# Seven block products for eight in twelve of the 22 up pairs of a feed-forward

## The chip, the cores and the metric

The kernel runs on one core of a Trainium2 chip. The metric is the device time of one execution in microseconds; the median of three runs is 1257.51 us (1257.15 to 1257.99).

## The reference, cut to what matters

A gated-linear-attention block with its own feed-forward and norm comes first; then two layers on 256 latent and 256 context tokens of width 1024, each an attention mixer and a gated feed-forward, both modulated by six vectors that are made from the conditioning. Weights and activations are fp32. The change lies in the feed-forward of the first of these two layers (layer 0), which runs over both token sets, and in the last modulation set of layer 1.

```python
FFN_HIDDEN = ((8 * D_MODEL + 2) // 3 + 255) // 256 * 256      # 2816

def swiglu_ffn(h, w_in, w_out):
    a, g = jnp.split(h @ w_in, 2, axis=-1)
    return (jax.nn.silu(a) * g) @ w_out

for i in range(DEPTH_2):
    mod_l = (silu_c @ ada_w[i] + ada_b[i])[:, None, :]
    mod_c = (silu_cc @ ada_w[i] + ada_b[i])[None, None, :]
    ...
    h = h + g1_l * y_l
    h = h + g2_l * swiglu_ffn(ada_norm(h, norm_ffn[i], sh2_l, sc2_l), ffn_w_in[i], ffn_w_out[i])
    if ctx_out:
        hc = hc + g1_c * y_c
        hc = hc + g2_c * swiglu_ffn(ada_norm(hc, norm_ffn[i], sh2_c, sc2_c), ffn_w_in[i], ffn_w_out[i])
return rms_norm_2(h, norm_final)
```

## The kernel before

**Weights.** All weights stream through one list of units of 128 x 1024 numbers (512 KB), in the order in which they are used (`UNITS`). `w_load` issues their DMAs on SP into five `raw` buffers, four units ahead; `w_split` turns each into a high part `wh` (a cast on ScalarE, line 178) and a low part `wl` (a subtraction on VectorE, line 179), both fp32r, in twelve `w` buffers; `wnext` hands the next unit to the matmuls and splits up to `cap[0]` units ahead. Each product of two fp32 blocks is three fp32r matmuls (`mm3`, lines 193 to 195): high by high, low by high, high by low.

**Layer 0's feed-forward.** The hidden width 2816 is 22 blocks of 128. For each block f a pair of "f" units holds the columns of the a half and of the g half. `ffn_up` multiplies each unit, as the stationary operand, with the transposed tokens `fT` (256 latent columns, then 256 context columns): 8 blocks of K, three matmuls each, 512 columns. `ffn_act` makes silu(a) times g (lines 1111, 1112) and splits it (1118, 1119). `ffn_up_first` does the first two pairs in two halves of 256 columns. The 22 blocks go in two parts of 11; after each part `ffn_down0` multiplies them with the "h" units of the down matrix (two blocks of 128 rows by 512 columns; the eleventh block is a half unit) into one PSUM bank per token tile, and `gated` adds the result, times the gate, to the residual (1080, 1081). In the first part all four token tiles go together; in the second the context tiles (2, 3) come first and then, with the units loaded again, the latent ones (0, 1).

**Modulation.** `ada_jobs` makes the modulation vectors beside all this: each step loads 512 KB of `ada_w` into one of two `ada` buffers (line 304, on SP) and multiplies and sums it on VectorE (line 324), once per conditioning vector. `ada_run(adaC, n)` issues n steps. Sets 2 and 5 are gates, which `ada_finish` transposes on TensorE (348), stores as a row in DRAM and `load_gates` broadcasts back.

**Layer 1's feed-forward** runs on the latent tokens alone: in each of its turns `ffn_up` makes one pair of 256 columns and `mm_r` and `mm_h` one down unit of 512.

**Order.** The program is written in source order; outside the sections marked `manual_schedule` a planner sets the order on each engine, by source order and by what it takes to be ready, and may move independent steps ahead. On the chip each engine then keeps its order. A tile pool (`t2`, 58 buffers of 2 KB) holds nearly all else; PSUM has eight banks.

## Time and profile before

| | |
|---|---|
| median of three runs | 1257.51 us |
| the profiled execution | 1256.72 us, its span 1254.9 us |
| TensorE busy | 1244.0 us, 99% of the span |
| VectorE, ScalarE busy | 919.9 us (73%), 688.2 us (55%) |
| DMA | 231.22 MB, mean 184 GB/s |

The span runs from the first to the last instruction. Layer 0's feed-forward takes from about 575 to 940 us of it: up to 703 the first part's up pairs, to 760 its down products, to some 873 the second part's up pairs, then its down products. Matmuls are pipelined, so the duration shown for one (0.28 or 0.40 us) is longer than the step from its start to the next one's.

### The profile page before, as it was taken

To read this page: it belongs to the slowest core of one execution; us is meant where nothing else is said; L and a number is where in the kernel's file an instruction comes from. 1 tells how busy PE (TensorE), PEld (TensorE's weight loads), DVE (VectorE), ACT (ScalarE), POOL (GpSimd) and SP (SyncE) were. 2 spreads that over 40 slices of the span, in tenths; PEclk is the share of its full clock that TensorE was granted. 3 is DMA by queue.
4 is the path that set the end of the run, shared out by engine and by line. 5 is a ranking of instruction groups with operands and counts; after the bars stand their busy time and mean duration, and the time that the engine had idled before them with its cause. 6 is when DMAs were issued, how large, how long until landed. Compare 5 with 4: busy or idle time off the path is not lost.

```text
span 1254.9 us, 18667 instructions
## 1 busy us (share of the span) xinstructions
PE 1244.0 (99%) x6872; PEld 1043.2 (83%) x6872; DVE 919.9 (73%) x1638; ACT 688.2 (55%) x1344; POOL 78.7 (6%) x137
## 2 busy tenths in 40 slices
...
GB/s 304 189 151 237 192 289 268 271 277 246 198 249 111 105 110 118 160 197 118 213 177 206 259 266 249 205 100 102 197 204 76 113 84 131 219 187 185 186 185 34
DMA packets 68507, 231.22 MB, mean 184 GB/s; under 512 B 8048, under 2 KB 8736, under 8 KB 68416
## 3 DMA queue, kind: packets, MB, share of 16 engines
...
## 4 chain that ended last, share of the span: by engine, by line
PE 95%; ACT 2%; DVE 1%; issue 1%; DMA 0%; POOL 0%; SPq 0%; POOLq 0%; ACTq 0%
PE b L193 28%; PE b L194 28%; PE b L195 28%; PE b L1000 2%; PE b L1469 1%; PE b L981 1%; PE b L232 1%; PE b L1455 1%; PE b L562 1%; PE b L962 1%; PE b L963 1%; PE b L951 1%; PE b L1436 1%; DVE wl L179 0%; DMA t<-in_xt_dram 0%
## 5 line engine op out<-in xcount | busy, mean ns | idle before, releaser
L178 ACT CAST wh<-raw 128x1024 fp32r<-128x1024 f32 (+1 forms) x308 | 320.7, 1045 | 392.8 <-PE b L194 292.4
L179 DVE TENSOR_TENSOR wl<-raw,wh 128x1024 fp32r<-128x1024 f32 (+1 forms) x308 | 372.5, 1216 | 154.9 <-ACT wh L178 151.9
L193 PE MATMUL b<-t,wh 128*128 128x256 f32 (+1 forms) x1120 | 365.7, 327 | 0.0
L194 PE MATMUL b<-t,wl 128*128 128x256 f32 (+1 forms) x1120 | 365.6, 327 | 0.0
L195 PE MATMUL b<-t,wh 128*128 128x256 f32 (+1 forms) x1120 | 365.3, 327 | 0.0
L193 PE MATMUL b<-wh,t 128*128 128x512 f32 (+1 forms) x748 | 299.2, 402 | 1.2 <-ACT t L250 0.6
L194 PE MATMUL b<-wh,t 128*128 128x512 f32 (+1 forms) x748 | 294.8, 394 | 0.0
L195 PE MATMUL b<-wl,t 128*128 128x512 f32 (+1 forms) x748 | 294.7, 394 | 0.0
L193 PEld LDWEIGHTS b<-t,wh 128*128 128x128 f32 x1120 | 210.7, 188 | 22.2
L194 PEld LDWEIGHTS b<-t,wl 128*128 128x128 f32 x1120 | 210.8, 188 | 21.9
L195 PEld LDWEIGHTS b<-t,wh 128*128 128x128 f32 x1120 | 210.5, 188 | 20.4 <-DVE t L251 0.2
L195 PEld LDWEIGHTS b<-wl,t 128*128 128x128 f32 x748 | 140.4, 188 | 34.2
L193 PEld LDWEIGHTS b<-wh,t 128*128 128x128 f32 x748 | 140.4, 188 | 32.2 <-ACT t L250 1.0
L194 PEld LDWEIGHTS b<-wh,t 128*128 128x128 f32 x748 | 140.8, 188 | 30.1 <-DVE t L251 0.5
L324 DVE CUSTOM_DVE_ANT_0 a<-a,crow 128x1024 f32<-128x1024 f32 x96 | 117.6, 1233 | 28.8 <-DMA a<-in_ada_dram 28.3
L324 DVE CUSTOM_DVE_ANT_0 t<-a,crow 128x1024 bf16<-128x1024 f32 x64 | 78.5, 1237 | 7.3 <-DMA a<-in_ada_dram 7.1
L1112 DVE TENSOR_TENSOR t<-b,t 128x512 f32<-128x512 f32 (+1 forms) x42 | 23.7, 564 | 59.4 <-PE b L195 52.2
L205 POOL TENSOR_TENSOR c<-c,mhalf 128x1 f32<-128x1 f32 x21 | 14.2, 676 | 539.0 <-DVE c L204 538.9
L339 POOL TENSOR_TENSOR mod<-mod,bcol 128x8 f32<-128x8 f32 x20 | 13.4, 671 | 475.1 <-DVE mod L324 472.7
L1118 ACT CAST t<-t 128x512 fp32r<-128x512 f32 (+1 forms) x42 | 21.7, 516 | 28.6 <-DVE t L1112 28.6
L212 ACT ACTIVATE t<-t 128x512 f32<-128x512 f32 x40 | 24.8, 624 | 10.8 <-DVE t L1081 6.4
L1445 ACT ACTIVATE t<-b,c,c 128x512 f32<-128x512 f32 x32 | 26.0, 812 | 3.5 <-POOL c L1443 3.5
...
## 6 DMA issues: line engine op xcount, KB each, us to landing
raw<-in_wst_dram SPq DMA_DIRECT2D x310, 512.0 KB, 4.4
a<-in_ada_dram SPq DMA_DIRECT2D x96, 512.0 KB, 4.4
...
crow<-in_cvec_dram SPq DMA_DIRECT2D x2, 512.0 KB
```

The lines of the kernel that those rows point to most:

```text
L178: A.copy(out=h[:, :n], in_=raw[:, :n])
L179: V.tensor_tensor(out=l[:, :n], in0=raw[:, :n], in1=h[:, :n], op=ALU.subtract)
L193: T.matmul(o, lhsT=lh, rhs=rh, start=first, stop=False)
L194: T.matmul(o, lhsT=ll, rhs=rh, start=False, stop=False)
L195: T.matmul(o, lhsT=lh, rhs=rl, start=False, stop=last)
L205: G.tensor_tensor(out=ms[:, 3:4], in0=ms[:, 2:3], in1=mhalf[:, 0:1], op=ALU.pow)
L212: A.activation(out=junk[hf], in_=halves[hf], func=AF.Square, scale=1.0 / 32.0, accum_out=ms[:, hf:hf + 1])
L324: V.tensor_tensor_reduce(out=raw if ci == n_c - 1 else t2([D], BF16), in0=raw, in1=crow[ci], scale=1.0, scalar=0.0, op0=ALU.mult, op1=ALU.add,
L1000: T.matmul(po[e * 64:(e + 1) * 64, cols_], lhsT=v, rhs=probs[(head, "l" if lat_q else "c")][:, c, :], start=(c == 0), stop=(c == n_c - 1))
L1112: V.tensor_tensor(out=a, in0=pg_[:, :n], in1=a, op=ALU.mult)
L1118: A.copy(out=h, in_=a)
L1445: A.activation(out=pl, in_=sl, func=AF.Exp, scale=r, bias=mx[:, 1:2], accum_out=mx[:, 2:3])
```

## The change

The up products of pairs 10 to 21 are computed by Winograd's form of Strassen's scheme on a 2 x 2 by 2 x 2 grid: the a and the g unit are the two rows, the two halves of K the inner index, latent and context tokens the two columns. Seven products of block sums take the place of eight products of blocks; a product is 4 blocks of K by three matmuls by 256 columns. `pair_sums` makes the sums of the weights one pair ahead and splits them; `token_sums` makes the sums of the tokens once, from the unsplit tokens that `to_T` now also keeps in `fX`; `ffn_up7` runs the seven products into three banks and combines them on ScalarE and VectorE. The tokens lie in two sets of tiles, `fL` and `fC`, so a plain pair becomes two runs of 256 columns. The 22 blocks go in three parts of 8, 8 and 6, without half units; two more rounds of gated sums follow from that, and 28 down units are loaded instead of 36. The steps of the sets in `adaC` are spread anew, and layer 1's set 5 (`adaD`) is made in the first turns of layer 1's down loop, with its gates loaded at f = 12. Not shown below: `mm3` gets a flag that lets a group of matmuls add onto an earlier one, and the width of a split is always 1024.

```diff
-HALF = NFT // 2
+PARTS = ((0, 8), (8, 16), (16, 22))
+F_SEVEN = 10
...
-    for part in range(2):
-        for f in range(part * HALF, (part + 1) * HALF):
+    for lo, hi in PARTS:
+        for f in range(lo, hi):
             u += [("f", "ffn_in0", P * f), ("f", "ffn_in0", FH + P * f)]
-        dn = [("h", "ffn_out0", part * HALF + f, 512 * h) for h in range(2) for f in range(0, HALF, 2)]
-        u += dn if part == 0 else dn + dn
+        dn = [("h", "ffn_out0", f, 512 * h) for h in range(2) for f in range(lo, hi, 2)]
+        u += dn if hi < NFT else dn + dn
...
+    def seven(u):
+        return u[1] == "ffn_in0" and u[2] % FH >= P * F_SEVEN
...
-        while wpos[1] < len(UNITS) and wpos[1] - wpos[2] + 1 < cap[0]:
+        while wpos[1] < len(UNITS) and wpos[1] - wpos[2] + 1 < cap[0] and not seven(UNITS[wpos[1]]):
...
-    adaC = ada_jobs([(0, 5, True), (1, 0, True), (1, 1, True)] + [(1, v, False) for v in (3, 4, 2, 5)])
+    adaC = ada_jobs([(0, 5, True), (1, 0, True), (1, 1, True)] + [(1, v, False) for v in (3, 4, 2)])
+    adaD = ada_jobs([(1, 5, False)])
...
-    fT = new_T2()
+    fL, fC = new_T(), new_T()
+    fX = [t2([2, S]) for _ in range(KD)]
     o_half(1, 2, hc, 1)
     xn = [normed(t) for t in hc]
     o_half(0, 0, lat, 0)
-    o_half(1, 0, lat, 0, lambda: to_T(xn, fT, S, mod(0, 1, 4), mod(0, 1, 3)))
+    o_half(1, 0, lat, 0, lambda: to_T(xn, fC, 0, mod(0, 1, 4), mod(0, 1, 3), [z[:, 1, :] for z in fX]))
...
-    def ffn_up(L, src, n):
+    def ffn_up(L, src, n, conv=iter(())):
         ps_ = []
         for _ in range(2):
             u = wnext(("f", f"ffn_in{L}"))
             o = bank()
-            for k in range(KD):
-                mm_f(o[:, :n], u, src, k, 0, n, k == 0, k == KD - 1)
+            for t, X in enumerate(src):
+                for k in range(KD):
+                    mm_f(o[:, t * S:(t + 1) * S], u, X, k, 0, S, k == 0, k == KD - 1)
+            run(conv, 2)
             ps_.append(o)
         return ffn_act(*ps_, n)
...
-                mm_f(os_[-1][:, S:N2], us[-1], src, k, S, S, k == 0, k == KD - 1)
-        to_T(xn, src, 0, mod(0, 0, 4), mod(0, 0, 3))
+                mm_f(os_[-1][:, S:N2], us[-1], fC, k, 0, S, k == 0, k == KD - 1)
+        to_T(xn, fL, 0, mod(0, 0, 4), mod(0, 0, 3), [z[:, 0, :] for z in fX])
...
+    sT = {}
+    def token_sums(j):
+        lo, hi, q = fX[j], fX[j + KD // 2], t2([2, S])
+        V.tensor_tensor(out=q[:, 1, :], in0=hi[:, 1, :], in1=lo[:, 1, :], op=ALU.subtract)
+        V.scalar_tensor_tensor(out=q[:, 0, :], in0=q[:, 1, :], scalar=-1.0, in1=lo[:, 0, :], op0=ALU.mult,
+                               op1=ALU.subtract)
+        V.tensor_tensor(out=lo[:, 1, :], in0=lo[:, 0, :], in1=lo[:, 1, :], op=ALU.subtract)
+        V.scalar_tensor_tensor(out=lo[:, 0, :], in0=q[:, 0, :], scalar=-1.0, in1=hi[:, 0, :], op0=ALU.mult,
+                               op1=ALU.subtract)
+        for z, names in ((q, (2, 1)), (lo, (4, 3))):
+            h, l = t2([2, S], F32R), t2([2, S], F32R)
+            A.copy(out=h, in_=z)
+            V.tensor_tensor(out=l, in0=z, in1=h, op=ALU.subtract)
+            for i, name in enumerate(names):
+                sT[(name, j)] = (h[:, i, :], l[:, i, :])
+    def pair_sums(f, got):
+        i = wpos[1]
+        assert UNITS[i] == ("f", "ffn_in0", P * f)
+        w_load(i + 4)
+        x, y = raws.pop(i), raws.pop(i + 1)
+        z = sb.tile([P, 1024], F32, tag="raw", bufs=5, name=nm("raw"))
+        wpos[1] += 2
+        a, b = slice(0, 512), slice(512, 1024)
+        def parts(r):
+            h = sb.tile([P, 1024], F32R, tag="w", bufs=NW, name=nm("wh"))
+            l = sb.tile([P, 1024], F32R, tag="w", bufs=NW, name=nm("wl"))
+            A.copy(out=h, in_=r)
+            V.tensor_tensor(out=l, in0=r, in1=h, op=ALU.subtract)
+            got.append((h, l))
+        parts(x)
+        yield
+        V.tensor_tensor(out=z[:, a], in0=x[:, a], in1=y[:, a], op=ALU.add)
+        V.tensor_tensor(out=z[:, b], in0=z[:, a], in1=y[:, b], op=ALU.add)
+        parts(z)
+        yield
+        V.tensor_tensor(out=y[:, a], in0=y[:, a], in1=y[:, b], op=ALU.add)
+        parts(y)
+        yield
+        V.tensor_tensor(out=x[:, a], in0=z[:, b], in1=x[:, b], op=ALU.add)
+        hl = sb.tile([P, 1024], F32R, tag="w", bufs=NW, name=nm("w"))
+        A.copy(out=hl[:, a], in_=x[:, a])
+        V.tensor_tensor(out=hl[:, b], in0=x[:, a], in1=hl[:, a], op=ALU.subtract)
+        got.append((hl[:, a], hl[:, b]))
+        yield
+    def splits(n):
+        for _ in range(n):
+            w_split(wpos[1] + 1)
+            yield
+    def ffn_up7(got, conv):
+        wpos[2] += 2
+        r, r23, r4 = bank(), bank(), bank()
+        c1, c2 = t2([2, S]), t2([2, S])
+        H = KD // 2
+        def prod(o, n, c, X, first=True):
+            h, l = got[n]
+            for j in range(H):
+                k = slice(c + j * P, c + (j + 1) * P)
+                mm3(o, h[:, k], l[:, k], *X(j), first and j == 0, j == H - 1, not first)
+        run(conv, 2)
+        prod(r[:, 0:S], 0, 0, lambda j: fL[j])
+        A.copy(out=c1[:, 0, :], in_=r[:, 0:S])
+        prod(r23[:, 0:S], 0, 512, lambda j: fL[H + j])
+        got[0] = None
+        V.tensor_tensor(out=c1[:, 0, :], in0=r23[:, 0:S], in1=c1[:, 0, :], op=ALU.add)
+        run(conv)
+        prod(r[:, 0:S], 1, 512, lambda j: sT[(2, j)], False)
+        A.copy(out=c1[:, 1, :], in_=r[:, 0:S])
+        A.activation(out=c1[:, 0, :], in_=c1[:, 0, :], func=AF.Silu)
+        prod(r23[:, S:N2], 2, 512, lambda j: sT[(4, j)])
+        run(conv)
+        prod(r[:, 0:S], 1, 0, lambda j: sT[(1, j)], False)
+        got[1] = None
+        A.copy(out=c2[:, 0, :], in_=r[:, 0:S])
+        V.tensor_tensor(out=c2[:, 1, :], in0=c1[:, 1, :], in1=c2[:, 0, :], op=ALU.subtract)
+        V.tensor_tensor(out=c2[:, 0, :], in0=r23[:, S:N2], in1=c2[:, 0, :], op=ALU.add)
+        V.tensor_tensor(out=c2[:, 0, :], in0=c2[:, 0, :], in1=c1[:, 0, :], op=ALU.mult)
+        prod(r4[:, 0:S], 3, 0, lambda j: fC[H + j])
+        V.tensor_tensor(out=c2[:, 1, :], in0=r4[:, 0:S], in1=c2[:, 1, :], op=ALU.add)
+        prod(r[:, 0:S], 2, 0, lambda j: sT[(3, j)], False)
+        V.tensor_tensor(out=c2[:, 1, :], in0=r[:, 0:S], in1=c2[:, 1, :], op=ALU.add)
+        A.activation(out=c2[:, 1, :], in_=c2[:, 1, :], func=AF.Silu)
+        V.tensor_tensor(out=c2[:, 1, :], in0=r[:, 0:S], in1=c2[:, 1, :], op=ALU.mult)
+        a = c2.rearrange("p t s -> p (t s)")
+        h, l = t2([N2], F32R), t2([N2], F32R)
+        A.activation(out=h, in_=a, func=AF.Copy, scale=-1.0)
+        V.scalar_tensor_tensor(out=l, in0=a, scalar=-1.0, in1=h, op0=ALU.mult, op1=ALU.subtract)
+        return h, l
+    def ffn_down0(hf, uu, tiles, n_ada, between=None, conv=None):
         ac = {t: bank() for t in tiles}
-        for f2 in range(0, HALF, 2):
+        for f2 in range(0, len(uu), 2):
             u = wnext(("h", "ffn_out0"))
-            for j in range(min(2, HALF - f2)):
+            for j in range(2):
                 f = f2 + j
                 for t in tiles:
-                    mm_h(ac[t], u, j, uu[f], t, f == 0, f == HALF - 1)
-            ada_run(adaC)
-            if f2 == 4 and between is not None:
+                    mm_h(ac[t], u, j, uu[f], t, f == 0, f == len(uu) - 1)
+            if n_ada:
+                ada_run(adaC, n_ada)
+            if hf == 1 and len(sT) < 16:
+                token_sums(f2 // 2)
+            if conv is not None and f2 >= len(uu) - 4:
+                run(conv, 2)
+            if f2 == 2 and between is not None:
                 between()
         for t in tiles:
             gated((lat + hc)[t], ac[t], 0, t // 2, 5, hf)
...
-    for part in range(2):
+    got = []
+    for lo, hi in PARTS:
         uu = []
-        for f in range(HALF):
-            if part == 0 and f < 2:
-                uu += ffn_up_first(fT) if f == 0 else []
+        for f in range(lo, hi):
+            nxt = []
+            if f + 1 < hi:
+                conv = pair_sums(f + 1, nxt) if f + 1 >= F_SEVEN else iter(())
             else:
-                uu.append(ffn_up(0, fT, N2))
-            ada_run(adaC, 2)
-        if part == 0:
+                conv = splits(2) if f >= F_SEVEN else iter(())
+            if f < 2:
+                uu += ffn_up_first() if f == 0 else []
+            elif f < F_SEVEN:
+                uu.append(ffn_up(0, (fL, fC), N2, conv))
+            else:
+                uu.append(ffn_up7(got, conv))
+            got = nxt
+            if lo == 0:
+                ada_run(adaC, 2)
+        if lo == 0:
             load_gates(0, 5)
-            for hf in range(2):
-                ffn_down0(hf, uu, (2, 3, 0, 1))
+        if hi < NFT:
+            ffn_down0(0, uu, (2, 3, 0, 1), 3 if lo else 2)
+            got = []
+            ffn_down0(1, uu, (2, 3, 0, 1), 1 if lo else 0, None, pair_sums(hi, got) if hi >= F_SEVEN else None)
         else:
             for hf in range(2):
-                ffn_down0(hf, uu, (2, 3))
+                ffn_down0(hf, uu, (2, 3), 1)
             xn = [normed(t) for t in hc]
-            ffn_down0(0, uu, (0, 1))
+            ffn_down0(0, uu, (0, 1), 1)
             bT2 = new_T2()
             ada_run(adaC, 100)
             cap[0] = 7
-            ffn_down0(1, uu, (0, 1), lambda: to_T(xn, bT2, S, mod(1, 1, 1), mod(1, 1, 0)))
+            ffn_down0(1, uu, (0, 1), 0, lambda: to_T(xn, bT2, S, mod(1, 1, 1), mod(1, 1, 0)))
...
-    load_gates(1, 5)
...
         u = wnext(("r", "ffn_out1", f))
+        if f < 12:
+            ada_run(adaD)
+        if f == 12:
+            load_gates(1, 5)
...
```

## Rows read from the trace of the kernel before

**Rows 1.** The page's parts 1 and 4: busy time, and the chain that ended last.

```profile
PE 1244.0 (99%) x6872; PEld 1043.2 (83%) x6872; DVE 919.9 (73%) x1638; ACT 688.2 (55%) x1344; POOL 78.7 (6%) x137
...
PE 95%; ACT 2%; DVE 1%; issue 1%; DMA 0%; POOL 0%; SPq 0%; POOLq 0%; ACTq 0%
```

**Rows 2.** Windows by stage: length, busy us of each engine (instructions), clock, DMA share, GB/s.

```profile
575.00:703.00 128.00, 128.00 (x583) 104.40 (x583) 98.78 (x145) 39.29 (x50) 3.96 (x6) 1.00 0.64 200
703.00:760.00 57.00, 57.00 (x246) 45.86 (x245) 41.10 (x63) 11.65 (x12) 1.32 (x2) 1.00 0.77 253
760.00:860.00 100.00, 100.00 (x429) 80.34 (x428) 51.52 (x68) 28.72 (x38) 2.24 (x2) 1.00 0.54 174
860.00:940.00 80.00, 80.00 (x354) 64.49 (x353) 47.72 (x63) 35.19 (x52) 1.08 (x2) 1.00 0.59 180
...
1140.00:1254.00 114.00, 107.98 (x761) 100.45 (x759) 60.61 (x80) 46.99 (x70) 1.08 (x2) 1.00 0.48 145
```

**Rows 3.** Waits of TensorE over the span: engine, line, releaser, us, times, longest.

```profile
PE b L121 <- POOL mhalf L137: 1.3, 1, 1.3
PE b L193 <- ACT t L250: 0.6, 1, 0.6
```

**Rows 4.** Timeline of VectorE over one plain pair: start, us, instruction, idle before it.

```profile
825.10 0.69 DVE L1112 TENSOR_TENSOR t<-b,t 128x512 f32<-128x512 f32 x1 [3.57 <-PE b L195]
...
831.55 1.23 DVE L179 TENSOR_TENSOR wl<-raw,wh 128x1024 fp32r<-128x1024 f32 x1 [3.79 <-ACT wh L178]
836.35 0.69 DVE L1112 TENSOR_TENSOR t<-b,t 128x512 f32<-128x512 f32 x1 [3.57 <-PE b L195]
```

**Rows 5.** Timeline of TensorE in the last stage, around twelve 512-column products.

```profile
1121.00 0.28 PE L195 MATMUL b<-t,wh 128*128 128x256 f32 x1
1121.12 0.40 PE L193 MATMUL b<-wh,t 128*128 128x512 f32 x1
...
1123.93 0.28 PE L193 MATMUL b<-t,wh 128*128 128x256 f32 x1
...
1129.56 0.40 PE L193 MATMUL b<-wh,t 128*128 128x512 f32 x1
```

**Rows 6.** Timeline of VectorE where its instructions follow each other without a gap.

```profile
717.33 1.28 DVE L1080 TENSOR_TENSOR t<-b,t 128x512 f32<-128x512 f32 x2
718.53 1.28 DVE L1081 TENSOR_TENSOR t<-t,t 128x512 f32<-128x512 f32 x2
...
756.27 1.22 DVE L179 TENSOR_TENSOR wl<-raw,wh 128x1024 fp32r<-128x1024 f32 x1
757.41 1.22 DVE L324 CUSTOM_DVE_ANT_0 a<-a,crow 128x1024 f32<-128x1024 f32 x1
...
926.80 0.75 DVE L251 TENSOR_TENSOR t<-t,t 128x256 fp32r<-128x256 f32 x2
927.48 0.54 DVE L248 TENSOR_SCALAR t<-b,mod,mod 128x256 f32<-128x256 f32 x1
```

**Rows 7.** ScalarE: two rows of its timeline, then groups by shape (busy us, mean ns).

```profile
1121.20 1.05 ACT L178 CAST wh<-raw 128x1024 fp32r<-128x1024 f32 x1 [1.48 <-PE b L194]
1122.15 0.40 ACT L1118 CAST t<-t 128x256 fp32r<-128x256 f32 x1
...
L1462 ACT COPY t<-b 128x256 f32<-128x256 f32 x64 | 21.7, 403 | 2.8 <-PE b L1455 2.8
...
L1118 ACT CAST t<-t 128x512 fp32r<-128x512 f32 x22 | 13.7, 621 | 25.7 <-DVE t L1112 25.7
```

**Rows 8.** Timeline of VectorE: the reader of the products that end before 1121.12 us.

```profile
1121.39 0.42 DVE L1112 TENSOR_TENSOR t<-b,t 128x256 f32<-128x256 f32 x1 [0.70 <-PE b L195]
```

**Rows 9.** Waits of VectorE and of SP's queue from 575 to 935 us.

```profile
DVE a L324 <- DMA a<-in_ada_dram: 28.3, 19, 4.0
...
SPq L304 <- DVE mod L324: 104.4, 51, 4.8
```

**Rows 10.** DMA issues from 703 to 760 us: count, size, median us to landing.

```profile
a<-in_ada_dram SPq DMA_DIRECT2D x17, 512.0 KB, 4.3
raw<-in_wst_dram SPq DMA_DIRECT2D x11, 512.0 KB, 4.6
```

26 lines of the change are left out of this document (12 added, 14 removed).

## The prediction

> **What bounds the kernel now.** I read the page first, then the windows by stage, the waits of TensorE, and the timelines of a plain up pair. TensorE is busy for 99% of the span and 95% of the chain that ended last is its own work [rows 1]. In layer 0's feed-forward, from 575 to 940 us, it is busy for every microsecond, at the full granted clock [rows 2], and the list of what it waited for over the whole execution holds only sub-microsecond entries after the start, of which [rows 3] is the longest. So here a matmul taken away is time taken away, as long as what feeds TensorE keeps up. The feeders have room now: over 575 to 940 us VectorE is busy 98.8 + 41.1 + 51.5 + 47.7 = 239 of 365 us, 65%, and ScalarE 39.3 + 11.7 + 28.7 + 35.2 = 115 us, 32% [rows 2]. The reader should see that the change spends just this room.
>
> **The price of a product.** In the last stage, up and down products alternate without a gap [rows 5]. Twelve 512-column products run from 1121.12 to 1123.93, 0.234 us each; the 48 256-column products after them run to 1129.56, 0.1173 us each. A 256-column product is therefore half a 512-column one, within 1 ns: cutting products into blocks costs TensorE nothing in itself. A plain pair has 2 x 8 x 3 = 48 products of 512 columns, and pairs follow each other every 836.35 - 825.10 = 11.25 us [rows 4], again 0.234 us each.
>
> **The seven-product pairs on TensorE.** A pair now has 7 x 4 x 3 = 84 products of 256 columns: 84 x 0.1173 = 9.85 us, 1.40 us less than 11.25. Twelve pairs: -16.8 us. The eight plain pairs left (f = 2 to 9) are also cut into two 256-column halves, 96 x 0.1173 = 11.26 us: +0.1 us in all. The down products stay 22 x 4 x 2 x 3 = 528 of 512 columns in three parts instead of two. TensorE's floor for the change is **-16.7 us**.
>
> **What feeds them.** For VectorE I count steps from one start to the next, not durations: a 1024-element split takes 1.14 us, a 512-element operation 0.60, a 256-element one 0.34 [rows 6]. A plain pair costs it two splits and two 512-element operations, 3.48 us. A seven-product pair costs three full splits (3.42), four adds and the half split of 512 (3.00), seven combinations of 256 (2.38) and the last 512-element one (0.60): 9.40 us, against 9.85 on TensorE. VectorE thus goes to **95%** in these pairs. ScalarE gets three casts at 0.95, one of 512 elements (0.62), three copies out of PSUM (0.40), two Silus of 256, which I take at a copy's price, and one 512-element scaling (0.62): 6.1 us, 62% [rows 7]. Over the whole phase VectorE adds 12 x 5.92 = 71 us for the pairs, 4 x 2.56 = 10 for the token sums, 16 x 0.60 = 10 for the third part's gated sums; it loses 5 splits (36 down units, six of them halves, become 28), 6 us, and the eight moved modulation steps, 9 us. That is 239 + 76 = 315 us of some 349: 90%. By throughput it still fits, so what decides is whether each hand-over comes in time.
>
> **The hand-overs, a wait that before does not have.** Three of the seven products go on adding into bank r after ScalarE has copied it, so products 3, 5 and 7 each wait for a copy, with one other product (12 x 0.1173 = 1.41 us) between. A reader starts 0.39 us after the start of the last matmul it needs (1121.00, 1121.39) [rows 5, 8]; with a copy of 0.40 that is 0.79 us of the 1.41, so ScalarE may be 0.6 us late for free. A cast just begun (0.95) costs up to 0.3 us each time. Product 4 writes the other half of bank r23, whose first half VectorE reads for c1. If the two are kept apart, product 4 waits for a VectorE addition: 0.39 + 0.43 = 0.82 of 1.41 us. Ahead of that addition in VectorE's queue may stand one operation (free) or the first block of the next pair's sums, 1.14 + 0.60 + 0.60 + 1.14 = 3.48 us (not free). Behind a late addition stand the Silu on ScalarE, the copies behind that, and so TensorE again. Bounds per pair: below, nothing, since TensorE has no idle time that a block product could win back. Above: the last three VectorE steps of the pair before (1.28), the block (3.48) and the addition (0.43) end 5.2 us into the pair, where product 4 was due at 4.2: 1.0 us; with three late copies at 0.3, 1.9 us. I take **0.45 us**, nearer the lower end, because the sums of the next pair need only loaded weights and free buffers and may start before the pair does: +5.4 us for twelve.
>
> On this the Trainium skill (PSUM — Partial Sum Buffer, section "PSUM bank collisions raise a hardware error") speaks against the change: two engines may not touch one bank in the same partitions at once, even at different columns, and software has to order them. No row of before shows TensorE writing one half of a bank while the other is read, so nothing here confirms it; by it the wait of product 4 is certain, without it the wait falls away and the first rival below is the likeliest.
>
> **Modulation steps.** They wait for their loads: 28.3 us of VectorE's idle time in this phase, up to 4.0 us at once, and the loads themselves stand in SP's queue until VectorE frees one of their two buffers [rows 9]. The weight loads are queued behind them. Before, that cost TensorE nothing, since VectorE had 35% to spare; at 90 to 95% such a wait is paid more often. The steps are also packed closer: in part 1's first down half three per weight unit (5.63 us), in part 2 one per unit of 2.81 us. That is 1.4 us for each 512 KB load, where 703 to 760 us managed 28 loads, 2.04 us each [rows 10]. Sixteen loads would fall (2.04 - 1.41) x 16 = 10 us behind; four units loaded ahead and two converted ahead cover 6 x 2.81 = 17 us of it. So 0 to 10 us, and I take +1.5.
>
> **Costed at nothing.** Keeping the gates' rows allocates and moves no data. The last set's eight steps come into layer 1's down loop: eight loads, eight VectorE operations of 1.15 us, then one small addition, a transpose, a copy, a row store and two broadcasts issued on SP. VectorE is busy 60.6 of 114 us there and DMA 48% [rows 2]; the gates are asked for at f = 12 and first read after f = 21, nine turns of 8.44 us later. Without that cover each step would cost its 1.15 us or a wait of up to 4. The token sums have two plain pairs, 22 us, between them and their first use. The third part's added gated sums run beside down products.
>
> **Sum.** -16.7 + 5.4 + 1.5 = -9.8 us on the profiled execution, 1256.7 (its span of 1254.9 and 1.8 around it), which is 0.8 below the median of 1257.5. So 1246.9 there, and 1247.7 as a median.
>
> **The rivals.**
> *No hand-over is late* (0 to 0.15 us per pair): -16.7 to -14, 1241 to 1243.5. For it: 62% on ScalarE and 0.6 us to spare at each copy. Against it: VectorE at 95%, strictly in its written order. 0.22.
> *The forecast* (0.15 to 0.8 us per pair): 1243.5 to 1252.5. 0.48.
> *VectorE becomes the bound* (0.8 to 1.35 us): its 9.40 us plus about one wait for a load or for ScalarE per pair make 10.7 to 11.2 us, and most of the gain is eaten: 1252.5 to 1259. For it: the 95%, and [rows 9]. Against it: the pairs themselves issue no modulation step, unless some are ordered in among them. 0.18.
> *Slower: product 4 waits for VectorE's whole block in each pair.* Break-even is 16.7 / 12 = 1.39 us of TensorE idle per pair. At 1.9, the upper bound, the pairs cost +22.8: +7.6 with the loads, 1265. It needs the next pair's sums to start no earlier than the pair. The bank rule above is what makes this possible. 0.12.
> That the work is not saved at all I exclude: the count of products and their price are both certain.
>
> **How the numbers follow.** The likeliest case gives 1247.7; its own range is 1243.5 to 1252.5. The range for all runs from the floor, 1241, to 1257.5: it leaves out the slower case and the top of the third. A change within 0.2% (2.5 us) is about what a measurement of this kernel cannot tell from none. Faster than that means below 1255.0: 0.22 + 0.48 + 0.07 of the third = 0.77; within it 0.11; slower 0.12.
>
> **What the profile after would show.** Right: pairs 10.2 to 10.5 us apart instead of 11.25, about 84 products of 256 columns in each, VectorE above 85% between some 680 and 860 us, and TensorE for the first time idle there, some 5 us, before products 3, 4, 5 or 7, released by ScalarE's copies or VectorE's additions. The no-wait rival: pairs at 9.85 and no idle time. The slower one: TensorE idle over 1.4 us per pair, nearly all released by VectorE's addition into c1. I am wrong in another way if TensorE waits in the down parts, released by weight splits that stand behind a modulation step, or if the last stage's turns of 8.44 us grow.

## The result, and the profile after

The changed kernel takes 1262.42 us (median of five runs, 1260.85 to 1263.71) where the kernel before takes 1257.52 beside it: a ratio of 1.0038, interval 1.0023 to 1.0053. It is 0.38% **slower**. The forecast was 1247.7 us, and its range ended at 1257.5.

The profiled execution took 1261.52 us with a span of 1259.7, so 4.8 us more than before. The page's parts 1 and 4, beside [rows 1]:

```profile
PE 1238.2 (98%) x7688; PEld 1075.3 (85%) x7688; DVE 1001.5 (79%) x1814; ACT 719.3 (57%) x1416; POOL 77.8 (6%) x137
...
PE 80%; DVE 11%; DMA 3%; ACT 3%; issue 2%; POOL 0%; SPq 0%; POOLq 0%; DVEq 0%; ACTq 0%
```

TensorE's share of the chain fell from 95% to 80%; VectorE, its loads and ScalarE took it over. The windows of [rows 2], now of the changed kernel:

```profile
575.00:703.00 128.00, 128.00 (x902) 119.16 (x902) 105.11 (x159) 37.45 (x48) 5.26 (x6) 1.00 0.61 194
703.00:760.00 57.00, 53.34 (x428) 52.34 (x427) 55.81 (x95) 25.93 (x41) 0.00 (x0) 0.97 0.45 140
760.00:860.00 100.00, 97.71 (x616) 86.19 (x615) 90.11 (x149) 37.52 (x58) 0.72 (x3) 1.00 0.63 205
860.00:940.00 80.00, 75.47 (x470) 65.89 (x469) 66.59 (x106) 43.38 (x71) 2.04 (x3) 1.00 0.56 181
```

TensorE, which had no idle time here, now has 10.5 us of it, and VectorE is at 98% from 703 to 760 us. What TensorE waits for from 695 to 945 us (engine, line, releaser, us, times, longest), beside [rows 3]:

```profile
PE b L198 <- ACT t L1236: 3.8, 2, 3.5
PE b L198 <- DVE t L253: 1.2, 1, 1.2
PE b L198 <- ACT w L1212: 1.1, 1, 1.1
PE b L198 <- DVE t L1250: 1.0, 1, 1.0
PE b L237 <- DVE t L253: 0.9, 1, 0.9
PE b L198 <- ACT wh L1197: 0.8, 2, 0.6
PE b L199 <- DVE w L1213: 0.7, 2, 0.5
```

L1236 is the first copy out of bank r; L1212 and L1213 split the last weight sum; L1250 is a combination; L253 belongs to the transposes at the layer's end. Most of it is VectorE's work, or ScalarE's behind VectorE.

**The account.** I took the time from each matmul's start to the next one's, less its price (0.1175 us for 256 columns, 0.2344 for 512). From 690 to 960 us this excess was 1.7 us before and is 21.7 now: 11.4 up to 800, 4.5 up to 900, 5.8 up to 960. With the 16.8 us of products saved, and 1.2 us more lost elsewhere (0.8 of it in the last stage), that gives -16.8 + 20.0 + 1.2 = +4.4, of 4.8 us by which the spans differ. So the products are really saved, and more than that is lost in waits.

**The first pair.** The largest single loss is at product 3 of block 10. TensorE's timeline:

```profile
721.73 0.28 PE L198 MATMUL b<-t,w 128*128 128x256 f32 x1
725.50 0.38 PE L198 MATMUL b<-t,wh 128*128 128x256 f32 x1 [3.49 <-ACT t L1236]
725.72 0.28 PE L199 MATMUL b<-t,wl 128*128 128x256 f32 x1
```

ScalarE just before (start, us, instruction, idle time before it and what ended it):

```profile
720.33 0.63 ACT L1125 CAST t<-t 128x512 fp32r<-128x512 f32 x1 [5.89 <-DVE t L1119]
...
722.66 1.99 ACT L1197 CAST wh<-raw 128x1024 fp32r<-128x1024 f32 x2 [1.22 <-DVE raw L1204]
724.56 0.61 ACT L1125 CAST t<-t 128x512 fp32r<-128x512 f32 x1
725.08 0.36 ACT L1236 COPY t<-b 128x256 f32<-128x256 f32 x1
```

The copy L1236 stands in ScalarE's queue behind the casts (L1125) of the two plain pairs, each behind VectorE's multiplication L1119, and behind two casts of weight sums (L1197), which wait for VectorE's addition L1204. The last link is L1204: the second multiplication ends at 723.8 us, while the two casts keep ScalarE busy up to 724.6. VectorE reached all of these late, with no idle time since 695 us:

```profile
714.19 0.70 DVE L1180 TENSOR_TENSOR t<-t,t 128x512 fp32r<-128x512 f32 x1
714.79 1.30 DVE L1086 TENSOR_TENSOR t<-b,t 128x512 f32<-128x512 f32 x2
...
719.59 0.71 DVE L1119 TENSOR_TENSOR t<-b,t 128x512 f32<-128x512 f32 x1
...
721.92 0.71 DVE L1204 TENSOR_TENSOR raw<-raw,raw 128x512 f32<-128x512 f32 x1
...
723.12 0.71 DVE L1119 TENSOR_TENSOR t<-b,t 128x512 f32<-128x512 f32 x1
```

Token sums end at 714.8 us, the part's gated sums follow, and only then come the first plain pair's multiplication and the next weight sums. After 3.7 us without products the granted clock falls (windows of one microsecond; the number after POOL's is the clock):

```profile
726.00:727.00 1.00, 1.00 (x10) 1.00 (x10) 1.00 (x3) 0.70 (x2) 0.00 (x0) 0.89 0.56 98
727.00:728.00 1.00, 1.00 (x6) 1.00 (x6) 1.00 (x2) 0.38 (x1) 0.00 (x0) 0.50 0.73 283
```

That is 1.2 GHz for 2.4. Sixteen products come 0.213 us apart, which costs 16 x 0.0955 = 1.5 us, so this place costs 5.2 in all.

**The pairs.** VectorE over one of them, from one addition into c1 to the next, without idle time; beside [rows 4, 6]:

```profile
753.66 0.43 DVE L1239 TENSOR_TENSOR t<-b,t 128x256 f32<-128x256 f32 x1
753.99 0.70 DVE L1203 TENSOR_TENSOR raw<-raw,raw 128x512 f32<-128x512 f32 x1
754.59 1.23 DVE L329 CUSTOM_DVE_ANT_0 a<-a,crow 128x1024 f32<-128x1024 f32 x1
...
758.75 1.22 DVE L329 CUSTOM_DVE_ANT_0 a<-a,crow 128x1024 f32<-128x1024 f32 x1
...
765.38 0.41 DVE L1239 TENSOR_TENSOR t<-b,t 128x256 f32<-128x256 f32 x1
```

11.72 us, which is the predicted 9.40 plus two modulation steps of 1.145: the planner had moved them up from the down parts. Within the two parts the pairs are 11.7 to 15.1 us apart by this addition, not 10.2 to 10.5, and seven of these ten intervals hold two steps. TensorE is idle for little of that, for it meanwhile runs products of the next pairs and of the down part.

### The profile page after: what moved, and what is told of

It is laid out like the page before. It is cut to its first block, busy times and chain, and to the rows that moved or that the text cites. A ratio compares the mean times of both kernels' runs of the same rounds, so it can differ in the third digit from the quotient of the medians.

```text
span 1259.7 us, 20570 instructions
## 1 busy us (share of the span) xinstructions
PE 1238.2 (98%) x7688; PEld 1075.3 (85%) x7688; DVE 1001.5 (79%) x1814; ACT 719.3 (57%) x1416; POOL 77.8 (6%) x137
## 4 chain that ended last, share of the span: by engine, by line
PE 80%; DVE 11%; DMA 3%; ACT 3%; issue 2%; POOL 0%; SPq 0%; POOLq 0%; DVEq 0%; ACTq 0%
PE b L198 23%; PE b L199 23%; PE b L200 23%; DMA a<-in_ada_dram 3%; PE b L1006 2%; DVE a L329 2%; DVE wl L180 1%; DVE wl L1198 1%; PE b L1601 1%; PE b L987 1%; PE b L1587 1%; DVE t L1086 1%; PE b L237 1%; DVE t L1087 1%; PE b L568 1%
## 5 line engine op out<-in xcount | busy, mean ns | idle before, releaser
L179 ACT CAST wh<-raw 128x1024 fp32r<-128x1024 f32 x276 | 289.3, 1053 | 269.0 <-PE b L199 220.4
L180 DVE TENSOR_TENSOR wl<-raw,wh 128x1024 fp32r<-128x1024 f32 x276 | 336.2, 1228 | 125.7 <-ACT wh L179 124.1
L198 PE MATMUL b<-t,wh 128*128 128x256 f32 (+1 forms) x1344 | 393.8, 294 | 4.7 <-ACT t L1236 3.8
L199 PE MATMUL b<-t,wl 128*128 128x256 f32 (+1 forms) x1344 | 392.3, 292 | 0.0
L200 PE MATMUL b<-t,wh 128*128 128x256 f32 (+1 forms) x1344 | 391.2, 292 | 0.0
L198 PEld LDWEIGHTS b<-t,wh 128*128 128x128 f32 x1344 | 253.5, 189 | 16.3 <-ACT t L1236 4.2
L199 PEld LDWEIGHTS b<-t,wl 128*128 128x128 f32 x1344 | 254.0, 189 | 7.6
L200 PEld LDWEIGHTS b<-t,wh 128*128 128x128 f32 x1344 | 253.5, 189 | 5.8 <-DVE t L256 0.2
L329 DVE CUSTOM_DVE_ANT_0 a<-a,crow 128x1024 f32<-128x1024 f32 x96 | 117.7, 1233 | 9.1 <-DMA a<-in_ada_dram 8.7
L329 DVE CUSTOM_DVE_ANT_0 t<-a,crow 128x1024 bf16<-128x1024 f32 x64 | 78.8, 1238 | 12.1 <-DMA a<-in_ada_dram 11.9
L1197 ACT CAST wh<-raw 128x1024 fp32r<-128x1024 f32 x36 | 37.6, 1050 | 33.8 <-PE b L199 17.9
L1198 DVE TENSOR_TENSOR wl<-raw,wh 128x1024 fp32r<-128x1024 f32 x36 | 43.9, 1224 | 1.7 <-ACT wh L1197 1.6
L1119 DVE TENSOR_TENSOR t<-b,t 128x256 f32<-128x256 f32 (+1 forms) x30 | 15.4, 515 | 27.8 <-PE b L200 23.6
```

Source lines behind the costliest of these rows:

```text
L179: A.copy(out=h[:, :n], in_=raw[:, :n])
L180: V.tensor_tensor(out=l[:, :n], in0=raw[:, :n], in1=h[:, :n], op=ALU.subtract)
L198: T.matmul(o, lhsT=lh, rhs=rh, start=first, stop=False, skip_group_check=onto)
L199: T.matmul(o, lhsT=ll, rhs=rh, start=False, stop=False, skip_group_check=onto)
L200: T.matmul(o, lhsT=lh, rhs=rl, start=False, stop=last, skip_group_check=onto)
L329: V.tensor_tensor_reduce(out=raw if ci == n_c - 1 else t2([D], BF16), in0=raw, in1=crow[ci], scale=1.0, scalar=0.0, op0=ALU.mult, op1=ALU.add,
```

## The experiments

Three small edits come back in most kernels. "Own bank" gives product 4 a bank r3. "Wide" holds latent and context tokens side by side in one set of tiles again, so that a plain pair has 512-column products. F_SEVEN is the first block with seven products.

```diff
-        r, r23, r4 = bank(), bank(), bank()
+        r, r23, r3, r4 = bank(), bank(), bank(), bank()
...
-        prod(r23[:, S:N2], 2, 512, lambda j: sT[(4, j)])
+        prod(r3[:, 0:S], 2, 512, lambda j: sT[(4, j)])
```

```diff
-    fL, fC = new_T(), new_T()
+    fT = new_T2()
+    fL, fC = [[tuple(z[:, c] for z in p) for p in fT] for c in (slice(0, S), slice(S, N2))]
...
-                uu.append(ffn_up(0, (fL, fC), N2, conv))
+                uu.append(ffn_up(0, fT, N2, conv))
```

Ratios are to the kernel before, with their intervals. The seven-product kernels scatter, over 6.5 us in e2_own_bank, whose profiled execution was the slowest of its ten; so small differences of two such profiles say nothing.

### Is the loss in the pairs, or around them?

**e3_no_seven**: no seven-product pair and no sums.

```diff
-F_SEVEN = 10
+F_SEVEN = NFT
```

> All 22 pairs are plain (48 products of 512 columns, here cut into 96 of 256); no weight sums and no token sums; the three parts, the spread of the modulation steps and the moved last set stay. Theory A: without the pairs' extra work on VectorE the TensorE waits at 720 us and among the pairs go; what stays is the price of three parts and of the moves, the waits near 935 us included: 1257 to 1261 us. Theory B says the same of this run; it tells how much of the loss is not the pairs' at all.

Measured: 1262.68 us, ratio 1.0037 (1.0022 to 1.0052), 1.7 us above the expected range and the same as with all twelve pairs. So against pairs cut like these the twelve give back all that they save.

**e9_three_parts_wide**: as e3_no_seven, and wide.

> No seven-product pairs, and the plain pairs in products of 512 columns as before; the three parts, the spread of the modulation steps and the last set's move stay. If the halved products cost the 2 to 3 us by which their step exceeds half of a 512-column one (118.5 against 117.2 ns, times 1920 products), this comes to 1259 to 1260.5 us, and the rest, 2 to 3 us, is the shorter third part and the moved set. If halving costs nothing, it stays at 1262 to 1263 us.

Measured: 1258.94, ratio 1.0013 (1.0004 to 1.0022). Undoing the cut of the plain pairs' products gives back 3.7 us, or 3.0 by the ratios. Spread over the eighteen pairs that e3_no_seven cuts anew that is some 0.2 us each, but of the 4.3 us by which the two profiles differ only 2.2 lie between 575 and 960 us. In e3_no_seven the 256-column products come 118.4 ns apart from 590 to 640 us, in the changed kernel 117.3, the price of the prediction. So the changed kernel's six cut pairs cost between nothing and 1 us. The three parts, with the moved set, cost 0.13%, 1.6 us. Of the 4.8 us some 2 to 3 are then left to the seven-product pairs and what they do to the layer's end.

**e12_set_back**: as e9_three_parts_wide, with layer 1's set 5 made in layer 0's feed-forward as before.

```diff
-[(1, v, False) for v in (3, 4, 2)])
-    adaD = ada_jobs([(1, 5, False)])
+[(1, v, False) for v in (3, 4, 2, 5)])
...
-        if f < 12:
-            ada_run(adaD)
-        if f == 12:
-            load_gates(1, 5)
```

> All of the computation, no seven-product pair, plain pairs as whole 512-column products in three parts, as in e9_three_parts_wide, and the last modulation set made with the others in layer 0's feed-forward, as before. What is left of the change is the three parts with their extra gated sums. Theory (the moved set costs the last stage about 1.1 us, the three parts the rest of the 1.85 of e9_three_parts_wide): 1257.3 to 1258.3, the last stage as long as before. Rival (all of it is the three parts' joints, the moved set is free): 1258.6 to 1259.5. Second rival (the eight steps more in layer 0's feed-forward cost there what they save later): the same time, with the loss moved from the last stage to layer 0.

Measured: 1258.85, ratio 1.0013 (1.0004 to 1.0022). My theory fell, and the time is the first rival's. But the run doesn't test the move, for the planner had undone it: the last modulation sum starts at 788 us in e9_three_parts_wide and at 789 here. In the changed kernel, too, all are done before layer 1 begins (windows of L329 alone; the count has each sum and the reading of its result):

```profile
838.00:905.00 67.00, 8.61 (x14) 1.00 0.56 177
905.00:1259.00 354.00, 0.00 (x0) 1.00 0.45 143
```

TensorE's excess from 900 to 960 us is 3.8 us here and 3.7 in e9_three_parts_wide, against 2.2 before. The wait that goes with it, in the list of TensorE's waits from 695 to 960 us of e12_set_back:

```profile
PE b L237 <- DVE t L224: 0.7, 1, 0.7
```

L237 are the transposes of the layer's end. The last down half that covers the norm before them is now 3 units long instead of 6.

### What makes the pairs lose?

**e2_own_bank**:

> Product 4 gets a bank of its own, so it no longer shares one with the half that VectorE adds into c1; the work is otherwise the same. Theory A: VectorE's work is unchanged, 1259 to 1265 us, within 3 us of the changed kernel. Theory B: the wait before product 4 is gone, TensorE wins back most of its 12 to 14 us of waits among the pairs: 1247 to 1254 us.

Measured: 1255.04 us (1251.36 to 1257.88), ratio 0.9976 (0.9966 to 0.9985), 7.4 us below the changed kernel and 1 us above theory B's range, with all of the computation. Sharing the bank is thus dear, but not as I had it: in the changed kernel's trace one product 4 of twelve starts late, by 0.27 us. The written order of TensorE's instructions (in the built program; the trace doesn't name products) shows what the shared bank does: product 4 must stand between products 3 and 5, behind a wait for VectorE. In a bank of its own it is laid, like product 6, into the time in which the products on bank r wait for copies. The Trainium skill (PSUM — Partial Sum Buffer, section "PSUM bank collisions raise a hardware error") wants accesses of two engines to one bank ordered; the written wait is that order, and 7.4 us is its price here, paid in the order and not at the wait. The two profiles differ by 3.6 us only, so I can't say where all of the 7.4 lies. In them the own bank loses 2.5 us more at the first pair (715 to 740 us) and 6.0 less from 740 to 960.

**e1_short_mod** and **e6_short_bank**: 48 of the modulation steps beside layer 0's feed-forward sum 8 of 1024 columns (their loads remain; layer 1's set 5 stays whole), alone and with the own bank.

```diff
-V.tensor_tensor_reduce(out=raw if ci == n_c - 1 else t2([D], BF16), in0=raw, in1=crow[ci], scale=1.0,
+V.tensor_tensor_reduce(out=raw[:, c] if ci == n_c - 1 else t2([D], BF16)[:, c], in0=raw[:, c], in1=crow[ci][:, c], scale=1.0,
```

> The 48 modulation steps issued beside layer 0's feed-forward sum 8 of 1024 columns instead of all (their loads stay whole; the modulation values are therefore left incomplete). That takes 72 operations of about 1.0 us each, some 72 us, off VectorE in this phase. Theory A (VectorE has more work between 690 and 890 us than fits, because modulation steps are ordered in among the pairs): the pairs come 9.9 to 10.4 us apart and the time is 1241 to 1248 us. Theory B (product 4 waits for VectorE's addition out of the same bank, whatever else VectorE does): pairs stay above 11 us, time 1255 or more.

> Both at once: product 4 in a bank of its own, and the modulation steps beside layer 0's feed-forward summing 8 of 1024 columns (modulation values left incomplete). If the bank and VectorE's load are two causes that add up, this is 6 to 9 us below the changed kernel for the bank and another 4 to 5 for the steps: 1248 to 1252 us, with the wait before the first pair (some 5 us near 725 us) left. If the two are one cause, since the bank only passes on VectorE's lateness, it comes out like the better of the two alone: 1253 to 1256 us.

Measured: 1257.61, ratio 1.0005 (0.9996 to 1.0015), and 1255.32, ratio 0.9984 (0.9975 to 0.9993). Short steps help the changed kernel by 4.8 us and e2_own_bank by nothing: the two gains do not add up. The times are those of theory B and of one common cause. In e6_short_bank VectorE still waits for the loads of its short steps, ahead of the plain pair's multiplication (L1122 there):

```profile
722.24 0.17 DVE L332 CUSTOM_DVE_ANT_0 a<-a,crow 128x8 f32<-128x8 f32 x1 [2.43 <-DMA a<-in_ada_dram]
...
723.53 0.68 DVE L1122 TENSOR_TENSOR t<-b,t 128x512 f32<-128x512 f32 x1
```

**e14_no_steps**: own bank, and the 24 steps of sets 2 to 4 of layer 1 left out with their loads.

```diff
-[(1, v, False) for v in (3, 4, 2)])
+[])
```

> Product 4 in a bank of its own, as in e2_own_bank, and the 24 modulation steps of layer 1's sets 2, 3 and 4 left out with their loads (layer 1 reads other sets in their place); no step is left between the first part's down products and the end of layer 0's feed-forward. Theory (steps, and the waits for their loads, stand in VectorE's order among the pairs and make it late): no stall over 1 us at the first pair, the clock at 1.00 there, pairs 10.0 to 10.5 us apart, TensorE's loss from 690 to 800 us down from 11.9 us to under 4: 1245 to 1248.5. Rival (VectorE's 9.40 us per pair or ScalarE's order are enough by themselves): the stall stays above 3 us, and the time is 1252 to 1255.5.

Measured: 1251.10 us, ratio 0.9956 (0.9941 to 0.9971), between the two ranges. It is 4 us below e2_own_bank by the medians and 2.5 by the ratios, whose intervals just overlap. The excess from 690 to 800 us is down from 11.9 to 5.0. From 726 to 796 us VectorE still has 87% but TensorE idles for 0.2 us of 70 (windows of e14_no_steps):

```profile
695.00:726.00 31.00, 28.83 (x239) 28.45 (x238) 31.00 (x55) 14.09 (x21) 0.00 (x0) 1.00 0.22 69
726.00:796.00 70.00, 69.81 (x521) 65.47 (x520) 61.14 (x102) 35.90 (x59) 1.12 (x1) 1.00 0.51 166
```

So steps and loads among the pairs are a cause, though the profiles leave it in part open. Most of what the two profiles differ by, 4.5 of 7.0 us, is at the first pair, and there both kernels have just two steps (at 708 and 712 us, at 706 and 710), so it is the order around them that differs. From 726 to 796 us six steps remain here: with sets 2 to 4 gone they are layer 1's set 5, moved up from layer 1. In the third part, where no step is left, the loss from 840 to 905 us is 2.6 us, as in e2_own_bank with its steps (2.5). The first pair still stalls for 2.3 us, VectorE being full from 695 to 726.

**e13_no_token_sums** and **e19_neither**: own bank without the token sums; and without sums and steps.

> Product 4 in a bank of its own, as in e2_own_bank, and in addition the token sums left out: the seven products read unsummed tokens, so VectorE loses 16 operations of 512 and 8 of 512 for the low parts, about 10 us at 695 to 725 us, and ScalarE its 8 casts; nothing else changes. Theory (VectorE is behind when the seven-product pairs begin, because token sums, weight sums and gated sums meet there, and the first copy out of PSUM comes late by that): TensorE's stall before the first pair's product 3, 3.65 us in the changed kernel and 5.35 in e2_own_bank, falls under 1 us, the granted clock stays at 1.00 there, and the time is 1255.0 - 4.4 - 1 = 1249 to 1251. Rival (the stall is one of ScalarE's order or of loads, and the sums only lie beside it): the stall stays at 3.5 to 5.5 us and the time at 1254 to 1256.

> Product 4 in a bank of its own, the token sums left out as in e13_no_token_sums and the 24 modulation steps with their loads as in e14_no_steps; products read unsummed tokens, layer 1 other sets. Theory (the first pair's stall is VectorE's backlog from both together): no stall over 0.7 us there, the clock at 1.00, and 2.3 to 4 us less than e14_no_steps: 1247 to 1249. Rival (the first pair stalls by itself, for the weight sums of two pairs meet there): a stall of 2 us or more, 1250 to 1251.5.

Measured: 1255.68, ratio 0.9991 (0.9981 to 1.0000), and 1255.03, ratio 0.9982 (0.9973 to 0.9992); stalls of 4.7 and 3.6 us at the first pair. Both theories fell; the first run came out as its rival, the second is slower than either case. VectorE's timeline of e19_neither shows why leaving work out did not help:

```profile
713.40 1.23 DVE L329 CUSTOM_DVE_ANT_0 a<-a,crow 128x1024 f32<-128x1024 f32 x1 [2.91 <-DMA a<-in_ada_dram]
...
725.88 0.68 DVE L1119 TENSOR_TENSOR t<-b,t 128x512 f32<-128x512 f32 x1
```

The room is taken by steps that the planner moved there with the waits for their loads. They are layer 1's set 5, which the source places in layer 1's down loop: the other 24 steps of this kernel, 48 sums, are done by 703 us, and these eight are the last (windows of L329 alone; sums and their readings):

```profile
703.00:730.00 27.00, 9.74 (x16) 0.94 0.53 175
```

In e6_short_bank, e13_no_token_sums and here, the last plain pair's multiplication starts 1.7 us before the stall ends, and cast and copy follow it at once; in the changed kernel and in e2_own_bank the casts of the weight sums came between.

**e10_sums_later** and **e11_ten_sums_later**: own bank, the token sums beside plain pairs 8 and 9, with twelve and with ten pairs.

```diff
-            if hf == 1 and len(sT) < 16:
-                token_sums(f2 // 2)
...
+                if f in (8, 9):
+                    token_sums(2 * f - 16)
+                    token_sums(2 * f - 15)
```

> All of the computation. Product 4 in a bank of its own, twelve seven-product pairs, the token sums written after the plain pairs 8 and 9 (two sets of sums each) instead of among the first part's down products. Theory: VectorE has 10 us of token sums, 7 us of its own and the 9.4 us of the first pair's sums to do in the 22.5 us of two plain pairs, so it is still behind when the first seven-product pair begins: a stall of 2 to 6 us, the time 1253 to 1256. Rival (only the crowding with the gated sums of the first part's end matters): no stall over 1 us, 1249 to 1251.5.

> All of the computation. As e10_sums_later, with ten seven-product pairs instead of twelve (from block 12 on), so that the token sums have four plain pairs, 45 us, in which VectorE needs 14 for the pairs and 10 for the sums. The saving of the products is 10 x 1.40 = 14.0 us instead of 16.8. Theory (the stall at the first pair comes from VectorE's backlog): no stall over 1 us at the first pair, and the time is 1255.0 - 4.4 - 1 + 2.8 = 1251.5 to 1253.5, below e2_own_bank though two pairs fewer are saved. Rival (the first of these pairs stalls whatever stands before it): the stall stays at 3.5 us or more, the time 1256 to 1258.5.

Measured: 1261.77, ratio 1.0039 (1.0024 to 1.0054), and 1257.77, ratio 1.0002 (0.9993 to 1.0012). The first is slower than either of its cases: its profile has no single long stall, but waits of 1.3, 1.4 and 2.9 us at the first two pairs, mostly for casts and subtractions of the token sums (L1179, L1180), and 13.9 us of excess from 690 to 800. In e11_ten_sums_later the stall moves with the first pair, ends at 751 us and is 5.5 us long: the rival held. The stall goes with the passage from plain to seven-product pairs, not with 725 us. That it needs a plain pair ahead is likely, for e8_six_wide_bank (below), whose first such pair follows down products, has none, though its token sums and gated sums end just before, at 833 us.

**e18_act_later**: own bank; the last plain pair's `ffn_act` is written behind the next pair's addition into c1.

```diff
         V.tensor_tensor(out=c1[:, 0, :], in0=r23[:, 0:S], in1=c1[:, 0, :], op=ALU.add)
+        if due is not None:
+            due[-1] = ffn_act(*due[-1], N2)
```

> All of the computation. Product 4 in a bank of its own, as in e2_own_bank, and the last plain pair's Silu, multiplication and split written after the first seven-product pair's addition into c1, so that ScalarE's first copy stands ahead of the plain pair's cast. Theory (VectorE's backlog reaches TensorE at this one place, the cast that waits for the late multiplication with the copy queued behind it): the first stall falls from 5.35 us to under 1.5, the clock stays at 1.00, and the time from 1255.0 to 1249 to 1251.5. Rival (VectorE is late as a whole; what no longer waits at the copy waits at the next hand-over or in the next pair): the stall is spread over the first two pairs, 1253.5 to 1256.

Measured: 1254.19, ratio 0.9970 (0.9959 to 0.9982), the profiled stall 5.2 us. The theory fell; the time is the rival's, but the stall isn't spread, it stays whole in its place. The copy waits behind the casts of the next weight sums, which wait for VectorE, as they did in the changed kernel. ScalarE's timeline of e18_act_later:

```profile
725.22 1.99 ACT L1197 CAST wh<-raw 128x1024 fp32r<-128x1024 f32 x2 [1.79 <-DVE raw L1204]
727.12 0.36 ACT L1236 COPY t<-b 128x256 f32<-128x256 f32 x1
```

### Remedies

**e7_pool_bank**: own bank, and the additions L1207 and L1210 on GpSimd.

```diff
-        V.tensor_tensor(out=y[:, a], in0=y[:, a], in1=y[:, b], op=ALU.add)
+        G.tensor_tensor(out=y[:, a], in0=y[:, a], in1=y[:, b], op=ALU.add)
```

> Own bank for product 4, and two of the four weight additions of each pair (the two that do not feed a first part) on GpSimd instead of VectorE: 1.2 us per pair less on VectorE, 9.40 to 8.20, all work kept. Theory A (VectorE's load): with about two modulation steps per pair VectorE comes to 10.5 us instead of 11.7, and the time is 1248 to 1253 us. If GpSimd's additions are late themselves or slow VectorE down: 1255 us or more.

Measured: 1267.83, ratio 1.0086 (1.0069 to 1.0103). GpSimd needs 2.1 and 1.7 us where VectorE needs 0.69, and VectorE's addition beside it is slower too (groups by shape of e7_pool_bank; us, mean ns):

```profile
L1207 POOL TENSOR_TENSOR raw<-raw 128x512 f32<-128x512 f32 x12 | 25.2, 2101 | 105.5 <-DVE raw L1203 48.8 <-issue 31.2 <-ACT t L1260 24.5
...
L1204 DVE TENSOR_TENSOR raw<-raw,raw 128x512 f32<-128x512 f32 x12 | 13.3, 1108 | 0.1
```

The addition L1204 takes a mean of 689 ns in e2_own_bank. By the Trainium skill (SBUF — State Buffer, section "Who interferes with whom") a VectorE instruction with two SBUF inputs and a GpSimd one that reads SBUF share a port, and one of them waits; the two means agree with that.

**e15_hold_steps**, **e16_six_wide_hold**, **e17_ten_hold**: each load of a step in the second and third part waits, by one element that GpSimd copies, for the last seven-product pair.

```diff
+                if hold:
+                    G.tensor_copy(out=loaded[n][:, 0:1], in_=hold[-1])
                 nc.sync.dma_start(out=loaded[n], in_=ada[(L * 6 + v) * KD + k])
```

> All of the computation. Product 4 in a bank of its own; each load of a modulation step in the second and third part waits, by one element that GpSimd copies from it, for the last seven-product pair made so far, so that the steps come beside the down products and not in among the pairs. Theory: no stall over 1 us at the first pair and pairs 10.0 to 10.6 us apart as in e14_no_steps, but in the second part's down products 16 steps of 1.145 us, 8 of them loads of 2 us or more in a row, beside gated sums and splits: some 1 to 4 us lost there: 1248 to 1252.5. Rival (the hold only moves the waits, since weights are queued behind the held loads): 1254 to 1260, with TensorE waiting for casts of weights in the down parts.

> All of the computation. As e8_six_wide_bank (six seven-product pairs, plain pairs of 512 columns, own bank), with the hold of e15_hold_steps, which acts on the eight steps of the third part alone. Theory: TensorE's loss from 800 to 900 us falls from 2.6 us to about 1, and the time from 1253.3 to 1251 to 1253. Rival (with six pairs the steps cost nothing): 1253 to 1254.5, or slower if the held steps come late for layer 1.

> All of the computation. As e15_hold_steps with ten seven-product pairs (from block 12 on), token sums in the first part's down products as in the changed kernel. The products saved fall from 16.8 to 14.0 us. Theory: without steps among the pairs VectorE keeps up with twelve as with ten, so this is e15_hold_steps plus 2.8: 1250.5 to 1255.5. Rival (VectorE is still late at the second part's start, where the sums of tokens and weights meet): two plain pairs more give it the time, and this is as fast as e15_hold_steps or faster.

Measured: 1275.23, 1271.40 and 1274.99; ratios 1.0139 (1.0122 to 1.0156), 1.0111 (1.0096 to 1.0126) and 1.0140 (1.0125 to 1.0155). The last of the held steps are too late for the layer's end, as in TensorE's waits of e15_hold_steps from 920 to 975 us, where the modulation's own transpose (L357) stands in TensorE's order:

```profile
PE b L357 <- POOL mod L348: 6.7, 1, 6.7
PE b L237 <- DVE t L224: 4.3, 1, 4.3
```

The first is slower than either of its cases, by another wait than the rival's; the second is the rival's slower case; that the third is as fast as the first says nothing, since both end on the late steps. Spreading the steps to where VectorE has room, by writing their places by hand, wasn't tried.

**e4_six** and **e8_six_wide_bank**: seven products in the third part's six pairs alone, the token sums in the second part's down products; the second also wide and with its own bank.

```diff
-F_SEVEN = 10
+F_SEVEN = 16
...
-            if hf == 1 and len(sT) < 16:
+            if hf == 1 and len(sT) < 16 and conv is not None:
```

> Only the six pairs of the third part are seven-product pairs; the token sums are made in the second part's second down half. TensorE's floor is six times -1.40, 8.4 us below the run without such pairs. Theory A: VectorE's first backlog (token sums, weight sums and two rounds of gated sums at 690 to 720 us) is gone, but pairs with modulation steps among them still run at VectorE's pace: 1251 to 1258 us. Theory B: each of the six pairs waits as before, about 1.3 us or more, and nothing is gained: 1257 to 1261 us.

> Six seven-product pairs (the third part only), own bank for product 4, and the plain pairs as before in products of 512 columns. Floor: 8.4 us below three parts with plain pairs. If halving the plain pairs' products cost 2 to 3 us, and the waits of the six pairs shrink to 2 us with the bank: 1252 to 1255 us. If neither matters: 1257 to 1259 us like the run with six pairs.

Measured: 1258.99, ratio 1.0011 (1.0002 to 1.0021), in theory B's range, and, as expected, **1253.25** (1252.83 to 1253.54), ratio **0.9968** (0.9955 to 0.9981). The second does all of the computation and beats both kernels, with half the pairs. TensorE's waits over its feed-forward are two, both at the layer's end. All its modulation sums start by 789 us, before the first seven-product pair, and from 838 to 905 us VectorE is 82% full, where the changed kernel's was at 90%:

```profile
838.00:905.00 67.00, 66.99 (x496) 62.32 (x495) 54.72 (x89) 37.07 (x59) 0.00 (x0) 1.00 0.45 141
```

Against e2_own_bank, with twelve pairs and a ratio of 0.9976 (0.9966 to 0.9985), it is not clearly faster. Twelve pairs that are also wide weren't run.

## Why the prediction was wrong

On its own execution the forecast was 1246.9 us and the time is 1261.52, 14.6 more. Three terms failed. Product 4's shared bank was priced as a wait, inside 0.45 us per pair; a bank of its own takes 7.4 us away, and the wait is hardly seen. The passage into the first pair was put at nothing; it costs 5.2 us here, and 3.7 to 8.2 in all the own-bank kernels with twelve pairs. VectorE's 9.40 us per pair left the modulation steps out; with two it needs 11.7. The rest held: behind the first pair, from 740 to 905 us, the profiles of e2, e6, e13, e14, e18 and e19 lose 3.8 to 6.4 us (e10_sums_later 7.9; the changed kernel 10.2), where I had 7.0. By the steps of the prediction:

- **TensorE's floor, -16.7: right as a count.** The account above closes with 16.8 us of products saved. Whether "cutting products into blocks costs TensorE nothing in itself" was right stays open: e3_no_seven against e9_three_parts_wide gives some 0.2 us per pair, about 1 us for the six that the change cuts anew where I had 0.1 in all, but the changed kernel's own profile shows none of it (excess of -0.1 us from 575 to 690).
- **The hand-overs, 0.45 us per pair: about right, and the smaller part.** The weight loads of products that add onto bank r wait for ScalarE's copies as described, but little (waits of the changed kernel from 575 to 945 us):

```profile
PEld b L198 <- ACT t L1248: 2.7, 11, 0.3
```

  This is 0.23 us per pair, inside the forecast. With the own bank a pair has two such hand-overs. One from e14_no_steps's third part, ScalarE's copy, then TensorE:

```profile
845.41 0.37 ACT L1242 COPY t<-b 128x256 f32<-128x256 f32 x1 [0.48 <-PE b L200]
...
845.57 0.28 PE L199 MATMUL b<-t,wl 128*128 128x256 f32 x1
845.84 0.38 PE L198 MATMUL b<-t,wh 128*128 128x256 f32 x1
846.06 0.28 PE L199 MATMUL b<-t,wl 128*128 128x256 f32 x1
```

  From the first of these matmuls to the third it takes 0.26 us more than their price. The next such place is 16 matmuls on: besides the 12 of product 5 the planner left only four before product 7, not the 12 of my 1.41 us. In e8_six_wide_bank nine of these make 2.4 of the 2.5 us that its six pairs lose from 840 to 905 us: 0.42 us per pair. The dear part in the changed kernel is another, near the one I had put among the rivals: VectorE late as a whole. From 690 to 900 us the pairs lose 11.1 us beside the first stall, against the 7.0 forecast for cuts, hand-overs and steps together.
- **"Against it: the pairs themselves issue no modulation step, unless some are ordered in among them."** They were: two in a pair, 11.7 us of VectorE for 9.85 of TensorE. This step failed in the pairs. The sum counted steps by their place in the source; the planner moves independent ones up. Taking most of them away with their loads gave 2.5 to 4 us (e14_no_steps), the larger part of it at the first pair, where I had charged 1.5.
- **"Costed at nothing": wrong.** The moved set never ran in layer 1's down loop, whose room I had counted for it: in the changed kernel the last modulation sum starts at 887 us. So the 9 us that I took off VectorE in layer 0 stayed there. The token sums were given 22 us of cover, the two plain pairs before their first use; in fact they fill VectorE to 100% from 695 to 726 us, together with the first part's gated sums and the first weight sums, and the copy behind them costs 3.65 us of idle TensorE and 1.5 of clock. VectorE's total was right, 318 us busy from 575 to 940 against the 315 forecast; its place was not. No wait of this size was in any of my cases. The third part's end costs 1.5 us by itself (e9_three_parts_wide, e12_set_back) and 3.7 in the changed kernel.
- **The rivals.** The pairs came out as in "VectorE becomes the bound": 16.3 us of excess more than before from 690 to 900 us, 1.36 us per pair, just past its 0.8 to 1.35, with 5.2 us of it at the first pair alone. The time lies above that case's 1259 by the third part's end and the last stage, which no case priced. "Product 4 waits for VectorE's block" named the right bank, worth 7.4 us, but not the way: product 4 is hardly seen to wait.
- **The loads on SP.** I had 0 to 10 us for them. VectorE's waits for them fell from 32.7 us (28.3 in [rows 9] and 4.4 for the first of two conditioning vectors) to 17.8:

```profile
DVE t L329 <- DMA a<-in_ada_dram: 9.1, 9, 3.4
DVE a L329 <- DMA a<-in_ada_dram: 8.7, 5, 3.7
```

  Yet a VectorE instruction that waits now stands ahead of work that TensorE needs, as here in the changed kernel:

```profile
784.93 1.23 DVE L329 CUSTOM_DVE_ANT_0 a<-a,crow 128x1024 f32<-128x1024 f32 x1 [3.68 <-DMA a<-in_ada_dram]
...
787.56 0.42 DVE L1250 TENSOR_TENSOR t<-b,t 128x256 f32<-128x256 f32 x1
...
788.03 0.50 PE L198 MATMUL b<-wh,t 128*128 128x512 f32 x1 [1.03 <-DVE t L1250]
```

What stays open: how much of VectorE's lateness at the first pair is the sums, the steps or the planner's order, since what was left out was replaced by other work moved up; what the steps among the later pairs cost by themselves; and where the 7.4 us of the own bank lie in full.
